# A hybrid attention and expert block on one core: low halves of the projection panels kept in DRAM, and two steps reordered

## Chip, cores and metric

The kernel runs on one core of one Trainium2 chip. The metric is the device time of one execution in microseconds; shown are single runs and their median.

## What is computed

One encoder layer on x of 1024 tokens by 1024 features, in f32, cut to what matters here:

```python
h = rms_norm(x, g_norm_mix) * (1 + sc1) + sh1
proj = h @ w_in                    # q, k, v of 8 FoX and 8 stick-breaking heads, forget logits
x = x + gt1 * (concat(norm(fox_attention), norm(sb_attention)) @ w_out)
h2 = rms_norm(x, g_norm_ffn) * (1 + sc2) + sh2
# PEER: 8 heads, per head two top-16 lists over 128 keys, then the top 16 of their sums
x = x + gt2 * sum(gelu(h2 . expert_down[e]) * gate * expert_up[e])
out = rms_norm(x, g_final)
```

## The kernel before, in words

**Two blocks and two parts.** Tokens are worked in two blocks: block A has 5 tiles of 128 tokens (in parts of 2 and 3 tiles), block B has 3. The front part (up to about 1215 us of the span) computes the adaptive weights, the projections, both attentions, the output projections and the PEER routing. The dense part (the rest) computes the experts: for block A's tokens all 128 x 128 experts as dense matmuls, for block B's tokens by gathering each token's chosen expert rows with indirect DMAs, in the background.

**Weights in two halves.** Each matmul against a weight is three matmuls (`mm3`, lines 379 to 381), of a rounded high half and the remainder. A weight panel, 128 x 1024 f32 (512 KB), is loaded as `wf` (line 329), ACT rounds it to `wh` (line 337), and DVE computes `wl = wf - wh` (line 344). Class `Panels` does this one panel ahead: `get` returns the pair that is ready, starts the next panel's rounding, puts its subtraction off by one step of the merge, and loads one more. The 24 panels of `w_in` are walked twice, by `proj(bA)` and by `proj(bB)`, so each is loaded, rounded and subtracted twice. The output and query panels (`w_out`, `w_q`) are split once, and both halves go to DRAM (line 347), from where block B reads them back (`Kept`, line 369).

**What sets the order.** In the front, Python generators yield costs, and `mrg` takes the one that is least far on, cost divided by a given total; a planner of the framework then orders each engine's instructions by the order of this code and by a timeline that it simulates. Around the change: `proj(bA)` and then `proj(bB)` (together `pp`) run as background beside the preparation of block B, attention A and the output projection of A, and after that in front, with A's routing `rA` behind. Then attention B (weight 70) and the rest of `rA` (weight 60) run beside each other. Last, output projection, routing of block B and the build of dense gates for one tile (`gbuild`).

**The attention.** `attention` (from line 580) waits until the first head pair is projected, loads its q, k and v from DRAM (lines 588 to 607), and then, turn by turn, computes scores (lines 641 to 644), softmax and stick-breaking steps on DVE and ACT, and the weighted sum (line 706).

**The dense part.** PE, DVE and ACT keep the written order there. Three expert chunks are loaded first (lines 1270 and 1272, on SP), then a chunk's down weights are split on ACT and DVE (`split_d`, lines 1289 and 1292), multiplied (`gelu_s`), weighted by the gates, and multiplied with the up weights (lines 1333 to 1335), in groups of four chunks. Between these, `sp_(n)` takes n steps of the background generator `sparse`. Its first steps are block B's candidate selection (`cands`, from line 930), three groups of 12 steps: the first seven of a group run from the copy of the indices (line 936) over eight rounds of top-16 (lines 958 to 962) to the position arithmetic (line 978); they are DVE instructions and two ACT casts (line 941). After the three groups come the gathers on POOL (lines 1221 and 1234). `PUMP_0` is 7:

```python
    for _ in range(WB):
        nextload()
    sp_(PUMP_0)
    nxt = ready.pop(0)
    split_d(nxt, True)
    split_d(nxt, False)
    gcur = loadg(0)
```

Of the kernel before, what the change touches and what calls it, by code (L numbers as in the profile page):

```python
# [11 lines left out]
F32 = mybir.dt.float32  # L12
F32R = mybir.dt.float32r
# [3 lines left out]
AF = mybir.ActivationFunctionType  # L17
# [3 lines left out]
P = 128  # L21
T = 1024
D = 1024
# [27 lines left out]
PUMP_0 = 7  # L51
# [31 lines left out]
WLP = 0  # L83
# [22 lines left out]
def tile_kernel(ctx: ExitStack, tc: tile.TileContext, x, ccol, w_ada, badac, bgt2, gcols, w_in, w_f, bf_, gout,  # L106
                w_out, w_q, keysT, edown, eup, wdense, gfin, out, dbg=None, stop=None):
    nc = tc.nc
    V, S, G, PE = nc.vector, nc.scalar, nc.gpsimd, nc.tensor
    dma = nc.sync.dma_start  # L110
# [3 lines left out]
    dram = ctx.enter_context(tc.tile_pool(name="dram", bufs=1, space=bass.MemoryType.DRAM))  # L114
# [31 lines left out]
    ksp = dram.tile([8, 2, P, T], F32R, name="ksp")  # L146
    vsp = dram.tile([8, P, T], F32, name="vsp")
    wsp = dram.tile([24, 2, P, D], F32R, name="wsp")
    gd = dram.tile([NPT * P // SB, P, NE * SB], F32, name="gd")
    gds = [dram.tile([NE * P * P, 1], F32, name="gds%d" % i) for i in range(2)]  # L150
    pidx = cst.tile([P, 1], F32, name="pidx")
# [2 lines left out]
    class Block:  # L154
        def __init__(self, t0, parts):
            self.t0, self.parts = t0, []
            i0 = 0
            for n in parts:
                self.parts.append((i0, n))
                i0 += n  # L160
            self.nt = i0
            self.ht = i0 * P
            self.nk = (t0 + i0) * P
            self.nq = 2 if t0 else 1
# [3 lines left out]
    def cols(i0, n):  # L168
        return slice(i0 * P, (i0 + n) * P)
# [70 lines left out]
    def defer(fn, n=1):  # L240
        t_ = [n, fn]
        late.append(t_)
        return t_
# [69 lines left out]
    def split(dst_h, dst_l, src):  # L313
        S.activation(dst_h, src, AF.Copy)
        V.tensor_sub(dst_l, src, dst_h.bitcast(F32))

    class Panels:
        def __init__(self, pool, srcs, bufs=3, eng=V, keep=None):
            self.eng, self.keep = eng, keep and list(keep)
            self.pool, self.src, self.bufs = pool, list(srcs), bufs  # L320
            self.ld, self.sp = [], []
            for _ in range(bufs - 1):
                self.load()
            self.split()

        def load(self):
            if self.src:
                w = self.pool.tile([P, D], F32, name="wf", tag="wf", bufs=self.bufs)
                dma(w, self.src.pop(0))
                self.ld.append(w)  # L330

        def split(self):
            if self.ld:
                w = self.ld.pop(0)
                wh = self.pool.tile([P, D], F32R, name="wh", tag="wh", bufs=2)
                wl = self.pool.tile([P, D], F32R, name="wl", tag="wl", bufs=2)
                S.activation(wh, w, AF.Copy)
                kp = self.keep.pop(0) if self.keep else None

                def low():  # L340
                    if self.eng is G:
                        G.tensor_sub(wl, w, wh.bitcast(F32))
                    else:
                        V.tensor_sub(wl, w, wh.bitcast(F32))
                    if kp is not None:
                        for n_, t_ in enumerate((wh, wl)):
                            dma(kp[n_].bitcast(F32), t_.bitcast(F32))

                self.sp.append((wh, wl, defer(low, LW)))
                self.load()  # L350
# [137 lines left out]
    def forget(b, hh, hl):  # L488
        wf = wp.tile([P, 64], F32, name="wff", tag="wff", bufs=1)
        dma(wf, w_f)  # L490
        wfh = wp.tile([P, 64], F32R, name="wfh", tag="wfh", bufs=1)
        wfl = wp.tile([P, 64], F32R, name="wfl", tag="wfl", bufs=1)
        split(wfh, wfl, wf)
        for i0, n in b.parts:
            w = n * P
            pf = pproj()
            mm3(pf[:NH, :w], wfh, wfl, hh, hl, cols(i0, n), NH)
            yield cyc(24 * w)
            fa = wp.tile([NH, HT], F32, name="fa", tag="pt", bufs=3)[:, :w]
            S.activation(fa, pf[:NH, :w], AF.Abs, bias=bft)  # L500
            S.activation(fa, fa, AF.Exp, scale=-1.0)
            S.activation(fa, fa, AF.Ln, bias=1.0)
            fm = wp.tile([NH, HT], F32, name="fm", tag="pt", bufs=3)[:, :w]
            V.tensor_scalar(fm, pf[:NH, :w], bft, 0.0, op0=OP.add, op1=OP.min)
            fc = wp.tile([NH, HT], F32, name="fc", tag="pt", bufs=3)[:, :w]
            t = b.t0 + i0
            V.tensor_tensor_scan(fc, fm, fa, 0.0 if t == 0 else fclast, op0=OP.add, op1=OP.subtract)
            if t + n < T // P:
                V.tensor_copy(fclast, fc[:, w - 1:w])
            dma(fcd[:, t * P:t * P + w], fc)  # L510
# [3 lines left out]
    done = set()  # L514

    def proj(b, hh, hl, pool):
        pan = Panels(pool, [w_in[j] for j in range(24)], bufs=2, eng=G if WLP else V)
        yield from forget(b, hh, hl)
        pend = []

# [9 lines left out]
        for pi in range(8):  # L530
            for s_ in range(3):
                wh, wl = pan.get()
                for i0, n in b.parts:
                    w, cs, gs = n * P, cols(i0, n), cols(b.t0 + i0, n)
# [45 lines left out]
    def attention(b, mixed, pool):  # L580
# [20 lines left out]
        def load_v(pi):  # L601
            vv = pool.tile([P, nk_], F32, name="vv", tag="vv")
            dma(vv, vsp[pi, :, 0:nk_])
            LV[pi] = vv
            LB[pi] = pool.tile([P, b.ht], F32R, name="qlb", tag="qlb", bufs=b.nq)
            for h_ in (la, lb):
                dma(LB[pi][h_].bitcast(F32), qsp[pi, 2, lb, qs_].bitcast(F32))
# [5 lines left out]
            yield -1  # L613
        load_kq(0)
        load_v(0)
        n = 8 * nt
        U = {}
        pair = {}
# [656 lines left out]
    def loadg(gi):  # L1275
        i1 = gi * CG
        dma = nc.sync.dma_start if gi > 1 else G.dma_start
        gg = dp.tile([P, CG, P], F32, name="gg", tag="gg", bufs=2)
        g2 = dp.tile([P, CG, P], F32, name="gg2", tag="gg2", bufs=1)
        for k in range(2):  # L1280
            dma((gg, g2)[k], gds[k].rearrange("(p c t) o -> p c (t o)", p=P, t=P)[:, i1:i1 + CG])
        g4 = dp.tile([P, NPT * P // SB, CG, SB], F32, name="g4", tag="g4", bufs=2)
        dma(g4, gd[:, :, i1 * SB:(i1 + CG) * SB].rearrange("s p (c t) -> p s c t", t=SB))
        return gg, g4, g2

    def split_d(k, act):
        if act:
            k.dh = dp3.tile([P, D], F32R, name="dh", tag="dh", bufs=2)
            S.activation(k.dh, k.wfd, AF.Copy)
        else:  # L1290
            k.dl = dp3.tile([P, D], F32R, name="dl", tag="dl", bufs=2)
            V.tensor_sub(k.dl, k.wfd, k.dh.bitcast(F32))  # L1292
# [63 lines left out]
    def sp_(n):  # L1356
        pump(n)
# [8 lines left out]

    for _ in range(WB):
        nextload()
    sp_(PUMP_0)
    nxt = ready.pop(0)  # L1370
    split_d(nxt, True)
    split_d(nxt, False)
    gcur = loadg(0)
    for gi in range(NG):
        grp = []
# [100 lines left out]
```

## Time and profile before

| | us |
|---|---|
| median of 3 runs (lowest, highest) | 3056.48 (3053.08, 3063.33) |
| the profiled execution | 3071.45 |
| its span, first to last instruction | 3069.7 |
| PE busy | 2895.8 (94%) |
| DVE busy | 2588.3 (84%) |
| ACT busy | 1189.7 (39%) |
| POOL busy | 1365.3 (44%) |

PE is the matmul engine TensorE, DVE VectorE, ACT ScalarE, POOL GpSimd, SP the queue that issues most DMAs. A time in a row is counted from the span's start. "[0.83 <-ACT qf L909]" behind an instruction says that its engine stood idle 0.83 us before it, until ACT's instruction of line 909 on tile qf let it go. L344 is line 344 of the kernel before.

### The profile page before, as it was taken

To read this page: it belongs to the slowest core of one execution; us is meant where nothing else is said; L and a number is where in the kernel's file an instruction comes from. 1 tells how busy PE (TensorE), PEld (TensorE's weight loads), DVE (VectorE), ACT (ScalarE), POOL (GpSimd) and SP (SyncE) were. 2 spreads that over 40 slices of the span, in tenths; PEclk is the share of its full clock that TensorE was granted. 3 is DMA by queue.
4 is the path that set the end of the run, shared out by engine and by line. 5 is a ranking of instruction groups with operands and counts; after the bars stand their busy time and mean duration, and the time that the engine had idled before them with its cause. 6 is when DMAs were issued, how large, how long until landed. Compare 5 with 4: busy or idle time off the path is not lost.

```text
span 3069.7 us, 48010 instructions
## 1 busy us (share of the span) xinstructions
PE 2895.8 (94%) x17472; PEld 2675.8 (87%) x17472; DVE 2588.3 (84%) x5282; ACT 1189.7 (39%) x2148; POOL 1365.3 (44%) x964
## 2 busy tenths in 40 slices
PE   5899998997989897889999999999999999999997
PEld 4899898997879897789898898998998989989986
DVE  6677554899997788889898998898989989989987
ACT  5566655445676763322132222231221222312212
POOL 0000000056756000055666665666666666666661
PEclk9999999998999998899999999999999999999998
DMA  7999454667435576379999999999999999999995
GB/s 256 285 346 280 142 198 177 211 183 197 105 82 165 217 266 241 104 277 354 350 354 339 334 355 338 344 361 347 343 344 332 346 345 342 364 332 343 340 328 196
DMA packets 368317, 856.93 MB, mean 279 GB/s; under 512 B 48952, under 2 KB 172880, under 8 KB 366032
## 3 DMA queue, kind: packets, MB, share of 16 engines
q1 hardware_dynamic: 236032, 440.08, 41.6%
q0 software_dynamic: 132048, 413.79, 38.3%
q8 instruction: 137, 2.24, 0.3%
q14 instruction: 100, 0.82, 0.1%
HBM read 742.49 MB, written 111.25 MB: 278 GB/s over the span
## 4 chain that ended last, share of the span: by engine, by line
PE 48%; DVE 22%; DMA 13%; issue 9%; ACT 4%; POOL 4%; SPq 0%; DVEq 0%; POOLq 0%; ACTq 0%
DMA ring<-in_eup,e 7%; PE sp L379 6%; PE sp L381 6%; PE sp L380 6%; DVE sacc L1239 4%; POOL ring L1234 3%; PE po L1333 3%; PE po L1335 3%; PE po L1334 3%; PE tp L1077 2%; PE av L706 2%; DMA wa<-in_w_ada 2%; PE proj L379 2%; PE pers L1333 2%; PE pers L1334 2%
## 5 line engine op out<-in xcount | busy, mean ns | idle before, releaser
L1234 POOL DMA_INDIRECT ring<-in_eup,e x384 | 557.5, 1452 | 289.7 <-DVE sacc L1239 150.3
L1221 POOL DMA_INDIRECT ring<-in_edown,e x384 | 519.2, 1352 | 373.3 <-DVE ring L1223 151.2
L379 PE MATMUL sp<-hT,dl 128*128 128x320 f32 x2048 | 636.5, 311 | 26.5 <-DVE dl L1292 16.1
L380 PE MATMUL sp<-hT,dh 128*128 128x320 f32 x2048 | 635.7, 310 | 0.0
L381 PE MATMUL sp<-hT,dh 128*128 128x320 f32 x2048 | 635.6, 310 | 0.0
L1239 DVE SCALAR_TENSOR_TENSOR sacc<-ring,sdot,sacc 128x1024 f32<-128x1024 f32 x381 | 488.2, 1281 | 66.8 <-DMA ring<-in_eup,e 62.2
L1223 DVE SCALAR_TENSOR_TENSOR ring<-ring,sx 128x1024 f32<-128x1024 f32 x384 | 460.7, 1219 | 67.2 <-DMA ring<-in_edown,e 66.1
L379 PEld LDWEIGHTS sp<-hT,dl 128*128 128x128 f32 x2048 | 387.1, 189 | 29.6 <-DVE dl L1292 15.3
L1297 ACT ACTIVATE uh<-wfu 128x1024 fp32r<-128x1024 f32 x128 | 134.8, 1053 | 680.3 <-PE po L1335 680.3
L380 PEld LDWEIGHTS sp<-hT,dh 128*128 128x128 f32 x2048 | 387.1, 189 | 1.2
L381 PEld LDWEIGHTS sp<-hT,dh 128*128 128x128 f32 x2048 | 387.0, 189 | 0.0
L1039 POOL DMA_INDIRECT gds<-g,e x128 | 238.5, 1863 | 263.0 <-DMA wf<-in_w_in 137.5
L1333 PE MATMUL po<-ul,ch 128*128 128x512 f32 x768 | 305.9, 398 | 21.1 <-DVE accB L1342 11.9
L1334 PE MATMUL po<-uh,ch 128*128 128x512 f32 x768 | 301.1, 392 | 0.0
L1335 PE MATMUL po<-uh,cl 128*128 128x512 f32 x768 | 301.1, 392 | 0.0
L1308 ACT ACTIVATE ge<-sp 128x320 f32<-128x320 f32 x256 | 110.4, 433 | 443.6 <-PE sp L381 443.5
L1333 PEld LDWEIGHTS po<-ul,ch 128*128 128x128 f32 x768 | 145.4, 189 | 66.0 <-DVE accB L1342 28.8
L1334 PE MATMUL pers<-uh,ch 128*128 128x512 f32 x512 | 199.6, 390 | 0.0
L1333 PE MATMUL pers<-ul,ch 128*128 128x512 f32 x512 | 199.5, 390 | 0.0
L1335 PE MATMUL pers<-uh,cl 128*128 128x512 f32 x512 | 199.2, 389 | 0.0
L303 POOL TENSOR_TENSOR i<-ms,mhalf 128x4 f32<-128x4 f32 (+1 forms) x16 | 22.4, 1400 | 338.7 <-DVE ms L301 338.7
L1335 PEld LDWEIGHTS po<-uh,cl 128*128 128x128 f32 x768 | 145.4, 189 | 31.2
(307 smaller groups left out, 6534.4 us busy)
## 6 DMA issues: line engine op xcount, KB each, us to landing
wfd<-in_wdense SPq DMA_DIRECT2D x128, 512.0 KB, 6.7
wfu<-in_wdense SPq DMA_DIRECT2D x128, 512.0 KB, 6.6
gd<-gt SPq DMA_DIRECT2D x16, 2048.0 KB, 8.3
g<-gd SPq DMA_DIRECT2D x30, 1024.0 KB, 14.9
wa<-in_w_ada SPq DMA_DIRECT2D x96, 256.0 KB, 5.3
wf<-in_w_in SPq DMA_DIRECT2D x48, 512.0 KB, 4.5
gds<-zt SPq DMA_DIRECT2D x32, 512.0 KB, 6.2
gg<-gds SPq DMA_DIRECT2D x60, 256.0 KB, 6.5
```

What stands on the lines that cost most here:

```text
L379: PE.matmul(pt, wl[:, c], hh[:, kd, cs], start=kd == 0, stop=False)
L380: PE.matmul(pt, wh[:, c], hl[:, kd, cs], start=False, stop=False)
L381: PE.matmul(pt, wh[:, c], hh[:, kd, cs], start=False, stop=kd == KD - 1)
L1039: G.indirect_dma_start(out=gds[nsct[0]], out_offset=off, in_=b.g[:, c_:c_ + 1], in_offset=None, compute_op=OP.add)
L1221: G.indirect_dma_start(out=r, out_offset=None, in_=edown, in_offset=bass.IndirectOffsetOnAxis(ap=bs.e[:, c_:c_ + 1], axis=0))
L1223: (V.scalar_tensor_tensor(r, r, 1.0, sx, op0=OP.mult, op1=OP.mult, accum_out=s_[:, j:j + 1]))
L1234: G.indirect_dma_start(out=r, out_offset=None, in_=eup, in_offset=bass.IndirectOffsetOnAxis(ap=bs.e[:, c_:c_ + 1], axis=0))
L1239: (V.scalar_tensor_tensor(acc, r, s_[:, j:j + 1], acc, op0=OP.mult, op1=OP.add))
L1297: S.activation(k.uh, k.wfu, AF.Copy)
L1333: PE.matmul(po, k.ch[:, tcs], k.ul[:, ds_], start=c == 0 and (gi == 0 or not per), stop=False)
L1334: PE.matmul(po, k.ch[:, tcs], k.uh[:, ds_], start=False, stop=False)
L1335: PE.matmul(po, k.cl[:, tcs], k.uh[:, ds_], start=False, stop=c == CG - 1 and (gi == NG - 1 or not per))
```

## The change

Three edits. First, a DRAM tensor `wlo` of 24 panels: in `proj(bA)` each low half is also written there after its subtraction; in `proj(bB)` the low half is loaded from there into `wl` (two buffers) beside the load of `wf`, and no subtraction is done; the rounding on ACT stays. Second, attention B yields a cost of 10 once, after its first loads and before its first scores. Third, the seven first background steps of the dense part come after the first chunk's split.

```diff
--- before.py
+++ after.py
@@ -146,6 +146,7 @@
     ksp = dram.tile([8, 2, P, T], F32R, name="ksp")
     vsp = dram.tile([8, P, T], F32, name="vsp")
     wsp = dram.tile([24, 2, P, D], F32R, name="wsp")
+    wlo = dram.tile([24, P, D], F32R, name="wlo")
     gd = dram.tile([NPT * P // SB, P, NE * SB], F32, name="gd")
     gds = [dram.tile([NE * P * P, 1], F32, name="gds%d" % i) for i in range(2)]
     pidx = cst.tile([P, 1], F32, name="pidx")
@@ -315,8 +316,9 @@
         V.tensor_sub(dst_l, src, dst_h.bitcast(F32))
 
     class Panels:
-        def __init__(self, pool, srcs, bufs=3, eng=V, keep=None):
+        def __init__(self, pool, srcs, bufs=3, eng=V, keep=None, lows=None, out=None):
             self.eng, self.keep = eng, keep and list(keep)
+            self.lows, self.out, self.wl = lows and list(lows), out and list(out), []
             self.pool, self.src, self.bufs = pool, list(srcs), bufs
             self.ld, self.sp = [], []
             for _ in range(bufs - 1):
@@ -328,13 +330,23 @@
                 w = self.pool.tile([P, D], F32, name="wf", tag="wf", bufs=self.bufs)
                 dma(w, self.src.pop(0))
                 self.ld.append(w)
+                if self.lows:
+                    wl = self.pool.tile([P, D], F32R, name="wl", tag="wl", bufs=2)
+                    dma(wl.bitcast(F32), self.lows.pop(0).bitcast(F32))
+                    self.wl.append(wl)
 
         def split(self):
             if self.ld:
                 w = self.ld.pop(0)
                 wh = self.pool.tile([P, D], F32R, name="wh", tag="wh", bufs=2)
+                if self.wl:
+                    S.activation(wh, w, AF.Copy)
+                    self.sp.append((wh, self.wl.pop(0), None))
+                    self.load()
+                    return
                 wl = self.pool.tile([P, D], F32R, name="wl", tag="wl", bufs=2)
                 S.activation(wh, w, AF.Copy)
+                lo_ = self.out.pop(0) if self.out else None
                 kp = self.keep.pop(0) if self.keep else None
 
                 def low():
@@ -342,6 +354,8 @@
                         G.tensor_sub(wl, w, wh.bitcast(F32))
                     else:
                         V.tensor_sub(wl, w, wh.bitcast(F32))
+                    if lo_ is not None:
+                        dma(lo_.bitcast(F32), wl.bitcast(F32))
                     if kp is not None:
                         for n_, t_ in enumerate((wh, wl)):
                             dma(kp[n_].bitcast(F32), t_.bitcast(F32))
@@ -514,7 +528,9 @@
     done = set()
 
     def proj(b, hh, hl, pool):
-        pan = Panels(pool, [w_in[j] for j in range(24)], bufs=2, eng=G if WLP else V)
+        low_ = [wlo[j] for j in range(24)]
+        pan = Panels(pool, [w_in[j] for j in range(24)], bufs=2, lows=low_ if b.t0 else None,
+                     out=None if b.t0 else low_)
         yield from forget(b, hh, hl)
         pend = []
 
@@ -613,6 +629,8 @@
             yield -1
         load_kq(0)
         load_v(0)
+        if b.t0:
+            yield 10.0
         n = 8 * nt
         U = {}
         pair = {}
@@ -1366,10 +1384,10 @@
 
     for _ in range(WB):
         nextload()
-    sp_(PUMP_0)
     nxt = ready.pop(0)
     split_d(nxt, True)
     split_d(nxt, False)
+    sp_(PUMP_0)
     gcur = loadg(0)
     for gi in range(NG):
         grp = []
```

## Rows read from the trace of the kernel before

**Rows 1.** The page's busy tenths in 40 equal slices, PE and DVE.

```profile
PE   5899998997989897889999999999999999999997
...
DVE  6677554899997788889898998898989989989987
```

**Rows 2.** By stretch: us, PE, PEld, DVE, ACT, POOL busy, PEclk, DMA share, GB/s.

```profile
140.00:260.00 120.00, 114.73 (x853) 112.46 (x852) 85.97 (x185) 78.17 (x185) 5.99 (x5) 1.00 1.06 338
...
580.00:690.00 110.00, 108.83 (x709) 108.25 (x707) 108.41 (x539) 49.42 (x112) 39.57 (x23) 1.00 0.62 190
...
690.00:930.00 240.00, 208.56 (x1424) 191.88 (x1424) 233.16 (x823) 159.13 (x333) 157.27 (x86) 0.90 0.50 123
...
1100.00:1200.00 100.00, 97.93 (x691) 97.08 (x689) 90.65 (x424) 53.66 (x86) 1.21 (x2) 1.00 0.68 250
...
1200.00:1320.00 120.00, 86.53 (x444) 78.85 (x444) 99.06 (x404) 36.57 (x50) 6.37 (x8) 0.84 0.37 125
```

**Rows 3.** Instructions on tile wl: the subtraction, ns min/median/max.

```profile
L344 DVE TENSOR_TENSOR wl<-wf,wh x72: 1199/1220/1230, 36.1 to 763.9; 128x1024 fp32r<-128x1024 f32 x72
```

**Rows 4.** Line 329's issues on SP, 565 to 660 us, ns; landing us.

```profile
L329 SPq DMA_DIRECT2D wf<-in_w_in x10: 328/332/333, 571.1 to 654.7; - x10
...
DMA to landing us min/median/max: 3.5/4.3/4.6
```

**Rows 5.** DMA, 140 to 260 us: packets, MB, share; count, KB, landing.

```profile
q1 hardware_dynamic: 43221, 40.37, 105.3%
...
wf<-in_w_in SPq DMA_DIRECT2D x10, 512.0 KB, 6.3
```

**Rows 6.** Waits of PE on DMA, 100 to 350 us: total us, times, longest.

```profile
PE sc L641 <- DMA qlb<-qsp: 2.5, 2, 1.4
```

**Rows 7.** ACT's timeline, last attention's start: start us, us, instruction [idle, releaser].

```profile
692.44 0.74 ACT L1016 ACTIVATE i2c<-bq 128x16 f32<-128x16 f32 x6 [3.99 <-DVE bq L999]
...
695.35 0.47 ACT L526 ACTIVATE vv<-proj 128x384 f32<-128x384 f32 x1
```

**Rows 8.** PE's timeline there; its first two rows bound one panel's 24 matmuls.

```profile
683.50 0.33 PE L379 MATMUL sc<-hT,wl 128*128 128x384 f32 x1
...
687.50 0.34 PE L381 MATMUL sc<-hT,wh 128*128 128x384 f32 x1
...
695.87 0.58 PE L379 MATMUL proj<-hT,wl 128*128 128x256 f32 x1 [6.38 <-ACT vv L526]
...
707.24 0.56 PE L641 MATMUL sc<-ka,qla 128*128 128x512 f32 x1 [2.05 <-DMA ka<-ksp]
...
712.54 0.76 PE L641 MATMUL sc<-kb,qlb 128*128 128x512 f32 x1 [3.67 <-DMA qla<-qsp]
```

**Rows 9.** DVE's timeline at the start of the dense part, same columns.

```profile
1215.79 0.27 DVE L978 SCALAR_TENSOR_TENSOR bq<-pos,bq 128x128 f32<-128x128 f32 x1
...
1217.48 0.28 DVE L890 FIND_INDEX8 i<-v,sr 128x8 uint32<-128x128 f32 x1
...
1226.15 1.23 DVE L1292 TENSOR_TENSOR dl<-wfd,dh 128x1024 fp32r<-128x1024 f32 x1 [8.39 <-ACT dh L1289]
...
1228.71 1.23 DVE L1292 TENSOR_TENSOR dl<-wfd,dh 128x1024 fp32r<-128x1024 f32 x1 [1.33 <-ACT dh L1289]
...
1255.42 0.69 DVE L1318 TENSOR_TENSOR ge<-ge,g 128x512 f32<-128x512 f32 x1 [3.23 <-ACT ge L1308]
```

**Rows 10.** SP's timeline there: the first dense load.

```profile
1217.79 0.33 SPq L1270 DMA_DIRECT2D wfd<-in_wdense  x1
```

**Rows 11.** DVE's timeline: third group's seven steps, and the split behind them.

```profile
1289.42 0.28 DVE L936 CAST ifl<-i 128x256 bf16<-128x256 uint32 x1
...
1306.34 1.22 DVE L1292 TENSOR_TENSOR dl<-wfd,dh 128x1024 fp32r<-128x1024 f32 x1
```

**Rows 12.** PE's timeline in the first dense group: its longest wait.

```profile
1288.70 0.80 PE L1333 MATMUL po<-ul,ch 128*128 128x512 f32 x1 [7.68 <-ACT accB L1340]
```

**Rows 13.** POOL's timeline: the gather from which they follow steadily.

```profile
1318.32 1.16 POOL L1221 DMA_INDIRECT ring<-in_edown,e  x1 [25.85 <-DVE g L1004]
```


## The prediction

> **What bounds the kernel now.** I read the page's busy slices first: TensorE (PE) is near full nearly everywhere and VectorE (DVE) joins it from the middle of the front part to the end [rows 1]. So the question for each stretch is which of the two has no slack, and the table of busy time by stretch answers it [rows 2]. From 140 to 260 us (projection of the first block) PE is busy 114.7 of 120 and DVE only 86.0: PE bounds, while the DMA share is 1.06, the fullest stretch outside the dense part. From 580 to 690 (projection of the second block beside routing of the first) both are full, 108.8 and 108.4 of 110. From 690 to 930 (last attention beside the rest of that routing) DVE is busy 233.2 of 240 and PE 208.6: DVE bounds. From 1100 to 1200 PE is at 97.9 of 100. At the start of the dense part, 1200 to 1320, PE falls to 86.5 of 120 and DVE does 99.1. The timelines of the two hand-overs that the change touches come next: into the last attention [rows 7, 8] and into the dense part [rows 9 to 13]. In both, PE waits for something that DVE or a queue is late with.
>
> The profiled execution took 3071.45 us (span 3069.7 and 1.75 around it), 15.0 above the median of 3056.48. The sum below is a difference, taken in that execution and added to the median. A measurement can tell about 0.3% from no change: 9 us.
>
> **Stores in the first block's projection.** Each of 24 panels now sends its low part, 512 KB, to DRAM. The subtraction stays. A store stands on SP's queue behind a new wait for that subtraction; behind it queue the next panel's load, the q, k and v spills, the adaptive weights' loads and the zero fills. Ten panel loads fall in the full stretch of 140 to 260 us, which moved 40.37 MB, 336 GB/s [rows 5]; ten stores are 5.2 MB, 15.6 us at that rate. That is the upper bound, if nothing else gives way; zero is the lower, since PE waited for DMA there only 2.5 us in 250 [rows 6]. Between them I take +4: a quarter, because PE's own waits for DMA are the nearest row, and zero fills, which nobody needs soon, share the queue and give way first. The other 14 stores meet a queue with room.
>
> Of the rate itself, the table's row shows 338 GB/s at a share above one. The Trainium skill, "DMA: Bandwidth & Descriptors", section "Bandwidth", gives 425 GB/s for a very large transfer by one core alone. By it 45.6 MB in 120 us, 380 GB/s, would still fit, the stores would cost nothing and the sum would come out 4 us lower; no stretch of this trace that I read goes that high, so the row decides.
>
> **Loads and the dropped subtraction in the second block's projection.** It removes 24 subtractions of 1.22 us each [rows 3], 1.15 from one start to the next when DVE is full, so 27.6 us of DVE work. It adds 24 loads of 512 KB on SP. The last ten panel loads of this projection go out from 571.1 to 654.7, 9.3 us apart, and land in a median of 4.3 [rows 4]. The loaded low part has two buffers, so the load for panel k+2 waits until panel k's last matmul, and has panel k+1's 9 us to land: cost nothing, covered by panel k+1; without that cover it is PE that waits.
>
> What the 27.6 us are worth depends on the place. The panels before 571 fall where DVE has room: nothing. The last ten, 11.5 us, fall where DVE is full [rows 2]. PE is full there too, so the projection can't end earlier. But at its end DVE is behind: ScalarE (ACT) waits 3.99 us for the route's indices on DVE, its copy of the last v comes at 695.35, and PE has stood 6.38 us for the buffer that this copy frees [rows 7, 8]. With 11.5 us less behind it DVE would have caught up. The last v, and with it the last attention's loads, can come 6.4 us sooner; the other 5 us come back only if DVE stays fed until 930. Bounds: 0 and -27.6. I take -10, nearest to the ten panels and a little less because the queue and ACT's order keep some.
>
> **The last attention's first turn.** Its loads are issued as before, but the merge books 10 units on it, of 70, so routing (60) gets 8.6 units first: about one panel. A panel's 24 matmuls of 384 columns run from 683.50 to 687.7, 4.2 us [rows 8], those of 256 two thirds of it: 7 us of PE put ahead of the first scores, with their DVE work behind. Nothing is added; what is moved issues no DMA but the panel's own load and spill. Today PE stands 3.67 us at the second half of the first scores for a load [rows 8]. Filling it is worth up to that; losing costs up to 7, the panel, if the attention's own chain ends the stage. I take -2, because DVE is the bound there and its order matters more than PE's.
>
> **The first dense split.** Seven steps of background work (candidate selection for one group) now come after the first split instead of before. Their DVE instructions run in written order. Before, they were mixed into the route's tail and the last ended at 1216 [rows 9], in a stretch that PE bounds [rows 2], so they cost nothing. Then DVE stood 8.39 us for the first dense weights, and the first split came at 1226.15 [rows 9]. It needs the load that goes out at 1217.79 [rows 10], just behind DVE's last route instruction [rows 9], and the change moves neither. After it, the seven steps stand bare between the first and the second split. The third group of the same work shows them alone: 1289.42 to 1306.34, 16.9 us [rows 11]. Cover: DVE's wait of 1.33 before the second split goes [rows 9]; the route's tail loses a handful of these instructions, about 1.2 us (four or five of 0.2 to 0.3 behind the last scores' arrival); and of DVE's later waits for PE, 3.23 the longest [rows 9], some 3.2 in all go. 16.9 - 1.3 - 1.2 - 3.2 = +11. PE's first chunk (48 matmuls) covers only part: it waits for the second split, and later 7.68 us on the same DVE chain as now [rows 12]. The steps' two ACT casts come behind the first split's and hold up nothing. POOL has none of it, but its steady gathers start only when DVE has done all three groups, at 1318.32 [rows 13], so they move by the same 11. Bounds: -1.2 (they still find a gap) and +16.9.
>
> Sum: +4 - 10 - 2 + 11 = +3, so 3059 us. The planner that orders the front's instructions can move each term by a few us.
>
> **Rivals.** (A) Slower: the relief doesn't reach the end. Place: the second block's projection, where PE is busy 108.8 of 110. Price: the dropped subtractions and the turn become 0, the sum is +4 + 11 = +15, 3071. It decides if the copy of the last v comes less than 3 us sooner, counted from the projection's last matmul. For it: PE shows no gap to win there. Against: the 6.38 us that PE stands right after it. (B) Faster: the stores cost nothing, all 11.5 us pass on, the attention's start gains its 6.4 on top, and the turn fills the 5.7 us that PE stands at the first scores (2.05 and 3.67 [rows 8]): 0 - 11.5 - 6.4 - 5.7 + 11 = -12.6, 3044. For it: DVE is the bound for 240 us after. Against: two of the gains may be the same time. (C) The change doesn't do what it says at the split: the steps still land in the route's tail, the sum is +4 - 10 - 2 - 1 = -9, 3047. Against it: the written order held in every case that I followed. (D) The low loads come late, 2 us for each of 24 panels: +48, 3104. Against it: 9.3 us between panels.
>
> **How the numbers follow.** Forecast 0.34, A 0.28, B 0.25, C 0.08, D 0.05. Within 0.3%: forecast and C, 0.42; faster by over 0.3%: B, 0.25; slower: A and D, 0.33. The range reaches below B and above A by some of the bounds of the stores and of the split, and leaves out D: 3038 to 3082. The likeliest case alone spans 3050 to 3066.
>
> **What would show it.** No subtraction in the second projection and DVE below 100 of 110 there; PE's stop after it shorter than 3 us; PE's DMA waits in the full stretch up by some us; the seven steps between the first and second dense split, and the first steady gather some 11 us later counted from the first split. It is wrong if the second split still follows the first within 3 us, if PE waits for low parts, or if DVE in 690 to 930 shows new idle time as large as the relief.

## The result, and the profile after

The changed kernel takes 3097.78 us (median, 3080.17 to 3099.24) against 3059.89 for the kernel before. The medians are 37.9 us apart and the means 34.0; the ratio on record for the comparison is 1.0095 (95% interval 1.0075 to 1.0116), so **slower by 29 us** (23 to 36), and all that follows goes by such ratios. 3059 was forecast, in a range that ended at 3082. The profiled execution took 3098.34 us (span 3096.5).

The table of busy time by stretch, after (us, then PE, PEld, DVE, ACT, POOL busy, granted clock, DMA share, GB/s), which answers [rows 2]:

```profile
140.00:260.00 120.00, 110.59 (x781) 105.89 (x782) 74.23 (x159) 63.50 (x151) 6.67 (x4) 1.00 1.04 342
...
580.00:690.00 110.00, 110.00 (x720) 109.83 (x720) 106.15 (x574) 52.84 (x122) 48.43 (x29) 1.00 0.78 238
...
690.00:930.00 240.00, 207.52 (x1376) 189.72 (x1376) 221.17 (x746) 153.18 (x318) 166.31 (x95) 0.89 0.51 120
...
1200.00:1320.00 120.00, 80.86 (x397) 74.08 (x398) 89.72 (x408) 34.58 (x47) 5.00 (x6) 0.79 0.34 111
```

In the second block's projection DVE fell from 108.4 to 106.2 and PE is full as before, 110.0 of 110. In the last attention and the rest of the routing, where DVE bounded with 233.2 of 240, it is now busy 221.2: 18.8 us of idle time where there were 6.8, at a granted clock of 0.89. That pair proves little, since the window is fixed and the attention's end is not. Two versions below whose code is that of the kernel before up to the tail of the route (the split's move alone, and the steps behind the second split) stood 13.1 and 16.9 us idle in it:

```profile
690.00:930.00 240.00, 213.77 (x1461) 197.19 (x1461) 226.95 (x782) 158.95 (x329) 154.84 (x85) 0.90 0.50 121
```

```profile
690.00:930.00 240.00, 215.70 (x1445) 199.79 (x1444) 223.12 (x750) 159.25 (x328) 156.55 (x87) 0.87 0.49 115
```

At the start of the dense part PE is busy 80.9 of 120 where it was 86.5, at a granted clock of 0.79.

The low parts do what they should. The instructions on tile wl, with ns least, median and most, answer [rows 3]:

```profile
L356 DVE TENSOR_TENSOR wl<-wf,wh x48: 1201/1224/1228, 36.6 to 738.3; 128x1024 fp32r<-128x1024 f32 x48
...
L358 SPq DMA_DIRECT2D wlo<-wl x24: 319/372/1130, 37.9 to 336.9; - x24
...
L335 SPq DMA_DIRECT2D wl<-wlo x24: 319/327/717, 342.9 to 659.8; - x24
```

24 of 72 subtractions are gone, 24 stores and 24 loads are there. ScalarE's timeline answers [rows 7]: the copy of the last v comes at 687.50, without a wait, 10.2 us after the projection's last matmul on a low half (677.3) where it came 14.4 after it (680.9 and 695.35). PE's stop of 6.38 us behind the projection is gone [rows 8]; its longest wait between 676 and 703 us is now 1.89.

```profile
687.50 0.47 ACT L542 ACTIVATE vv<-proj 128x384 f32<-128x384 f32 x1
```

DVE's timeline at the start of the dense part answers [rows 9]:

```profile
1212.12 0.68 DVE L904 MAX8 v<-scs 128x8 f32<-128x128 f32 x3 [11.34 <-ACT scs L897]
...
1226.64 1.23 DVE L1310 TENSOR_TENSOR dl<-wfd,dh 128x1024 fp32r<-128x1024 f32 x1 [7.41 <-ACT dh L1307]
...
1227.79 0.29 DVE L954 CAST ifl<-i 128x256 bf16<-128x256 uint32 x1
...
1244.50 0.29 DVE L996 SCALAR_TENSOR_TENSOR bq<-pos,bq 128x128 f32<-128x128 f32 x1
...
1244.78 1.23 DVE L1310 TENSOR_TENSOR dl<-wfd,dh 128x1024 fp32r<-128x1024 f32 x1
```

The route's tail has lost the seven steps and is no shorter for it: DVE stands 11.34 us for late scores, and the first split starts at 1226.64 (before: 1226.15). Then the steps stand bare from 1227.79 to 1244.78, and the second split is 16.1 us later than before. PE's timeline shows who pays, and POOL's (answering [rows 13]) that it lasts: the steady gathers start at 1334.91, 16.6 us later.

```profile
1227.92 0.63 PE L393 MATMUL sp<-hT,dl 128*128 128x320 f32 x1 [14.47 <-DVE dl L1310]
...
1246.15 0.61 PE L393 MATMUL sp<-hT,dl 128*128 128x320 f32 x1 [8.84 <-DVE dl L1310]
```

The first of the two waits was there before, the second is new:

```profile
1227.43 0.64 PE L379 MATMUL sp<-hT,dl 128*128 128x320 f32 x1 [15.16 <-DVE dl L1292]
```

POOL's row:

```profile
1334.91 1.17 POOL L1239 DMA_INDIRECT ring<-in_edown,e  x1 [25.87 <-DVE g L1022]
```

The spans differ by 26.8 us. The stretch from the first to the second split holds 15.6 of it, and 10.9 come between the ninth and the last split (1660.7 before, 1671.6 after). But that stretch is the same code in every kernel here with the old order at the split, and took 1660.7 to 1670.0 us in their profiles; in the three other versions with the steps between the splits it took 1663.5 to 1667.7. So most of the 10.9 is spread between executions, and **one pair of profiles can't say what the front did**: up to the last scores of the first attention five profiles of identical code end at 390.2 to 399.7 us, and the profile of before is the latest of them. That hides a loss in the front, which the experiments had to find by times. Below, a ratio is always to the kernel before in the same comparison, and 0.1% is 3.1 us.

### The profile page after: what moved, and what is told of

Same layout as the page of the kernel before. It is cut to its first block, busy times and chain, and to the rows that moved or that the text cites. A ratio compares the mean times of both kernels' runs of the same rounds, so it can differ in the third digit from the quotient of the medians.

```text
span 3096.5 us, 48074 instructions
## 1 busy us (share of the span) xinstructions
PE 2899.0 (94%) x17472; PEld 2671.7 (86%) x17472; DVE 2568.3 (83%) x5258; ACT 1186.3 (38%) x2148; POOL 1357.7 (44%) x964
## 3 DMA queue, kind: packets, MB, share of 16 engines
q0 software_dynamic: 132048, 413.79, 37.9%
## 4 chain that ended last, share of the span: by engine, by line
PE 44%; DVE 22%; DMA 13%; issue 11%; POOL 6%; ACT 5%; SPq 0%; DVEq 0%; POOLq 0%; ACTq 0%
DMA ring<-in_eup,e 7%; PE sp L393 4%; PE sp L394 4%; PE sp L395 4%; POOL ring L1252 4%; DVE sacc L1257 3%; PE proj L393 2%; PE proj L395 2%; PE proj L394 2%; PE tp L1095 2%; DMA ring<-in_edown,e 2%; PE av L724 2%; PE po L1351 2%; PE po L1352 2%; PE po L1353 2%
## 5 line engine op out<-in xcount | busy, mean ns | idle before, releaser
L1252 POOL DMA_INDIRECT ring<-in_eup,e x384 | 565.3, 1472 | 286.6 <-DVE sacc L1257 141.9
L1057 POOL DMA_INDIRECT gds<-g,e x128 | 223.6, 1747 | 226.5 <-DVE v L907 124.1
L1341 ACT ACTIVATE ch<-ge 128x640 fp32r<-128x640 f32 x128 | 94.5, 738 | 212.4 <-DVE ge L1336 199.6
L724 PEld LDWEIGHTS av<-vv,pt 128*128 128x128 f32 x1152 | 157.6, 205 | 17.6 <-ACT pt L738 10.3
```

Source lines behind the costliest of these rows:

```text
L724: m_ = PE.matmul(av_[:, a, i, :], pt[:, q * P:(q + 1) * P], vv[:, kb_ * P + a * 64:kb_ * P + a * 64 + 64], start=kb_ == 0, stop=kb_ == qt)
L1057: G.indirect_dma_start(out=gds[nsct[0]], out_offset=off, in_=b.g[:, c_:c_ + 1], in_offset=None, compute_op=OP.add)
L1252: G.indirect_dma_start(out=r, out_offset=None, in_=eup, in_offset=bass.IndirectOffsetOnAxis(ap=bs.e[:, c_:c_ + 1], axis=0))
```

## The experiments

**The parts of the change, each undone or alone.** Theory at this point: the moved steps are the whole loss. Rivals: the stores lose part of it in the front; the turn eats the relief. The steps put back ahead of the split:

```diff
         nextload()
+    sp_(PUMP_0)
     nxt = ready.pop(0)
     split_d(nxt, True)
     split_d(nxt, False)
-    sp_(PUMP_0)
```

> The changed kernel with the seven steps of background work put back ahead of the first dense split; stores, loads of low parts and the turn stay. Theory (the moved steps are the whole loss, 16.6 us bare between the first and second split, and the rest nets to nothing): second split again within 3 us of the first, first split within 4 us of 1226 us, time 16 to 28 us below the changed kernel, so within 9 us of the kernel before. Rival 1 (part of the loss is made in the front, by the stores): still 10 us or more above the kernel before, first split later than 1232. Rival 2 (the longer dense part, 1813 us from first to last split against 1786, is not the steps' doing): the dense part stays 10 us longer than before even with the second split within 3 us of the first.

Ratio 1.0038 (1.0022 to 1.0053), 11.6 us above the kernel before. The second split follows the first by 2.6 us. The split's part is 1.0095 - 1.0038, 17 us, and **the rest is not zero**: the theory falls. The first rival's time came, its sign did not: the first split is at 1221.0, not behind 1232. The second falls, as the way from the first split to the last is 6 us longer than in the profile before, not 10.

```diff
-        if b.t0:
-            yield 10.0
```

> The changed kernel without the turn booked on the last attention; stores, loads and the moved split stay. Theory (the last attention is bound by its own chain, the relief of VectorE becomes idle time there with or without the turn): first split within 4 us of 1226, time within 6 us of the changed kernel. Rival (the turn eats the relief, since it puts routing ahead of the attention that sets the end): first split 8 to 20 us sooner, before 1219, and the time lower by the same.

Ratio 1.0062 (1.0043 to 1.0080): 10 us below the changed kernel. The theory named 6, the rival a first split before 1219; it came at 1221.0. The turn costs. With both edits undone, only the stored low parts are left:

> Only the stored low parts: no turn, and the seven steps ahead of the first split as before. Theory (relief becomes idle time, the stores hide): within 6 us of the kernel before, the scores of the first attention some 9 us later as in the changed kernel and the first split within 4 us of 1226. Rival 1 (the relief is real and the turn ate it): 8 to 20 us below the kernel before. Rival 2 (the stores cost more than the loads give back): 5 to 15 us above it, with the first split later by that.

Ratio 1.0002 (0.9987 to 1.0017): stores and loads together are worth between 4 us less and 5 us more, as the theory had it by time. Its first split did not come within 4 us of 1226 but at 1215.9; the version above, whose code is the same up to there but for the tail, had it at 1221.0, so one profile says little here too. And the split's move alone, on the kernel before:

> The kernel before with the moved split alone, which is the seven steps behind the first dense split. Theory (the steps stand bare): second split 16 to 17 us later than the first's usual place, time 16 to 18 us above the kernel before; 25 to 28 above it if the later drift in the dense part is the steps' doing too. Rival (the move is hidden, the loss is made by the stores): within 5 us of the kernel before.

Ratio 1.0065 (1.0045 to 1.0085), 20 us (14 to 26): the theory's 16 to 18 lie in the interval, and the rival falls. Its DVE timeline, first and second split:

```profile
1219.99 1.23 DVE L1292 TENSOR_TENSOR dl<-wfd,dh 128x1024 fp32r<-128x1024 f32 x1 [7.11 <-ACT dh L1289]
...
1238.12 1.23 DVE L1292 TENSOR_TENSOR dl<-wfd,dh 128x1024 fp32r<-128x1024 f32 x1
```

18.1 us apart where 2.6 were: 15.5 of the 20 us are in sight there. From low parts alone to low parts and turn to the changed kernel the steps are +0.6, +11.0 and +17.4 us. These add up by construction; but in the other order the split costs 18.4 (the second of these runs less the third) and the turn 10.1.

**What the stores cost and the loads bring.**

```diff
-        low_ = [wlo[j] for j in range(24)]
+        low_ = [wlo[0]] + [None] * 23
...
-                     lows=low_ if b.t0 else None,
+                     lows=[wlo[0]] * 24 if b.t0 else None,
```

> No turn, the seven steps ahead of the first split as before. The first block's projection stores one panel's low part instead of 24, and the second block's projection loads that one for every panel, so its subtractions are gone and its loads are all there (which leaves the low parts of 23 panels out of the computation). Theory (the stores cost what the relief gives back): the first scores of the first attention come at 94 to 97 us as in the kernel before, and the time is 6 to 14 us below the kernel before. Rival (the relief is worth nothing, it turns into idle time of VectorE in the last attention): within 4 us of the kernel before.

Ratio 1.0003 (0.9986 to 1.0020), as the rival had it: what the loads free is, at best, a few us by the end.

```diff
-        pan = Panels(pool, [w_in[j] for j in range(24)], bufs=2, lows=low_ if b.t0 else None,
-                     out=None if b.t0 else low_)
+        pan = Panels(pool, [w_in[j] for j in range(24)], bufs=2, out=None if b.t0 else low_)
```

> No turn, steps as before; the first block's projection stores all 24 low parts and nobody reads them, the second block's subtracts as before. Theory (the stores delay the first block's first panels): first scores at 103 to 106 us, time 6 to 12 us above the kernel before. Rival (the stores are free by the end, the 9 us at the first scores are made up in the rest of the projection): within 4 us of the kernel before.

Ratio 1.0034 (1.0020 to 1.0049), 10 us, as the theory had it. The first scores come at 102.0 us (in the kernels without all stores 91.7 to 96.2, in those with them 102.0 to 105.7). But that is not a wait for the stores. The written order is another one: PE has 381 matmuls ahead of the first scores in every version with all the stores, and 325 in every version without. From the start to the first scores, stores alone and the kernel before (the last of its 326 is the first score):

```profile
0.00:102.00 102.00, 66.01 (x381) 55.27 (x382) 67.11 (x129) 53.80 (x105) 5.99 (x18) 0.97 0.83 288
```

```profile
0.00:94.90 94.90, 60.17 (x326) 50.16 (x327) 62.58 (x120) 48.02 (x94) 5.99 (x18) 0.93 0.77 263
```

In the stretch of 200 to 250 us, where the queue was full before, PE does 44.68 instead of 48.32 us while the rate is no higher (first the stores alone, then the kernel before); none of PE's waits there ends on a DMA.

```profile
200.00:250.00 50.00, 44.68 (x314) 42.32 (x314) 30.52 (x65) 26.28 (x62) 3.17 (x2) 1.00 1.03 335
```

```profile
200.00:250.00 50.00, 48.32 (x361) 47.50 (x360) 35.41 (x77) 32.23 (x80) 2.33 (x2) 1.00 1.06 348
```

```diff
-        low_ = [wlo[j] for j in range(24)]
+        low_ = [wlo[j] if j >= 12 else None for j in range(24)]
```

(and a panel without one is not loaded)

> Stored low parts for the last 12 of the 24 panels alone, where VectorE is full in the second block's projection; the first 12 are subtracted in both. No turn, steps as before. Theory (the stores' cost is made at the first panels, the relief at the last ten): first scores at 94 to 97 us, time 5 to 12 us below the kernel before. Rival (relief and cost are both spread evenly over the panels): half of each, within 4 us of the kernel before and of the version with all 24.

Ratio 0.9985 (0.9968 to 1.0002). The order ahead of the first scores is that of the kernel before again, they are back at 95.4, and the same stretch, in which this version's stores have begun, is at

```profile
200.00:250.00 50.00, 48.51 (x361) 47.52 (x360) 35.05 (x79) 32.11 (x80) 3.24 (x2) 1.00 1.05 353
```

so the cost goes with the stores of the first twelve panels. Whether these cost by the queue or by the order that the planner writes with them, no run here separates. Measured once more beside the next group:

> The version with the last 12 low parts stored, no turn, steps as before, once more, as the partner of the two versions above that are built on it. Theory (half the stores keep the relief and lose the cost): 2 to 10 us below the kernel before, again. Rival (it is the kernel before within the measurement): within 2 us of it.

Ratio 0.9973 (0.9954 to 0.9993). Over both, 5 to 8 us below the kernel before, at the theory's lower end, as if the relief were kept and the stores' cost lost. Against so plain a sum speaks that the loads alone gained nothing. The three full versions (1.0003, 1.0034, 1.0002) don't add up, by 10 us where their intervals allow some 8; the written order differs in each, and the next group shows what that alone is worth.

**The turn.** On the kernel before, alone:

> The kernel before with the turn alone. Theory (the turn puts some 8 us of routing ahead of the attention, which ends the stage, whether or not VectorE was relieved): 5 to 12 us above the kernel before, the scores of the last attention ending 4 to 9 us later counted from its first. Rival (the turn costs only with the relief, because then the routing runs out of work sooner): within 4 us of the kernel before.

Ratio 1.0022 (1.0007 to 1.0038), 7 us; from the last attention's first scores to its last 221.3 us where the kernel before had 208.0, more than the 4 to 9 us that were expected. The theory: it puts some 8 us of routing ahead of an attention that ends the stage. Two versions test that on the one with twelve low parts, where it takes 205.8 and 211.1 us:

```diff
-TOT_B = 70.0
+TOT_B = 80.0
```

> The version with the last 12 low parts stored, no turn, and the opposite of the turn: the last attention's total in the merge is 80 units instead of 70, so that it is put ahead of the routing by an eighth all along. Theory (the attention's own chain of turns ends the stage, what is put ahead of it costs and what is put behind it gains): the last scores 4 to 10 us sooner counted from the first ones, time 3 to 10 us below the version with 70. Rival (VectorE's sum of work is the bound, order costs only when the routing runs out too soon): the attention ends sooner and the routing's rest stands bare behind it, time within 4 us of the version with 70, or above.

```diff
+        if b.t0:
+            yield 20.0
```

> The version with the last 12 low parts stored, and a turn of 20 units instead of none (10 in the change). Theory (each 10 units put some 8 us of routing ahead of an attention that ends the stage): 14 to 22 us above the version without a turn, the last scores 15 to 25 us later counted from the first. Rival (a turn costs a fixed sum, by the panel put ahead of the first scores): 7 to 12 us above it, as with 10 units.

Ratios 0.9960 (0.9939 to 0.9980) and 0.9964 (0.9946 to 0.9983), beside 0.9973 for their partner. The first agrees with the theory, 4 us below its partner with the stage at 200.4 us, though intervals of 6 us can't tell it from its rival. The second was to lose 14 to 22 us, or 7 to 12 by its rival. **A turn of 20 units costs nothing, and the theory falls**, with that rival. What the stage shows instead is in its busy time. These are the windows from first to last scores: low parts alone, the same with the turn of 10, the kernel before with the turn of 10, and (a run below) the kernel before with 20:

```profile
701.80:912.60 210.80, 192.16 (x1296) 175.52 (x1296) 203.00 (x693) 144.64 (x291) 130.53 (x72) 0.90 0.50 123
```

```profile
699.60:915.90 216.30, 189.56 (x1253) 172.74 (x1254) 204.89 (x684) 142.84 (x292) 150.39 (x84) 0.88 0.51 120
```

```profile
701.00:922.30 221.30, 199.02 (x1265) 183.21 (x1266) 204.85 (x700) 144.68 (x296) 136.34 (x74) 0.85 0.48 118
```

```profile
706.50:901.50 195.00, 173.65 (x1237) 157.95 (x1235) 193.21 (x662) 142.94 (x284) 120.10 (x61) 0.96 0.51 128
```

DVE has 193 to 205 us of work in the stage; what it stands idle is 7.8, 11.4, 16.5 and 1.8 us, and the granted clock is 0.90, 0.88, 0.85 and 0.96. Differences of a few us are spread: the version with twelve low parts stood 5.2 and 10.0 us idle in two profiles of one code. The same order of the stage in other versions gives 10.4 beside the 7.8, 15.4 beside the 11.4, and 5.8 to 7.6 in three profiles of the kernel before's. From the longest of the four, windows around a fall of the clock:

```profile
830.00:840.00 10.00, 9.12 (x72) 8.02 (x70) 10.00 (x35) 7.13 (x12) 6.26 (x5) 1.00 0.86 208
...
840.00:844.50 4.50, 1.50 (x9) 1.02 (x9) 4.50 (x12) 2.61 (x5) 3.96 (x2) 1.00 0.61 180
...
844.50:865.00 20.50, 20.43 (x90) 19.85 (x91) 15.00 (x47) 11.54 (x27) 1.00 (x1) 0.50 0.02 1
```

PE was busy 9.12 of 10 us and then 1.50 of 4.5, with waits of 1.56 us at most; then the clock fell to 0.50, the lower of its two levels (1.2 GHz). For 20.5 us PE was busy nearly all the time at that speed, and DVE, the engine that bounds the stage, waited for it, as its timeline says:

```profile
860.77 0.56 DVE L674 TENSOR_SCALAR t<-sc 128x384 f32<-128x384 f32 x1 [3.27 <-PE sc L646]
```

The Trainium skill, "TensorE: Matmul & The Clock Gate", section "A second HAM failure mode: psum-queue depth-cycling", tells of a kernel whose TensorE stood often and briefly between groups of matmuls and swung between its two levels; the rows agree in that much. How much of the idle time the clock explains differs by version. On the kernel before with the turn of 10, 13.1 of DVE's 16.5 us fall while the clock is at the lower level; in the changed kernel only 4.7 of 15.4. So there the order makes DVE wait at the full clock too, and by what is not shown. Four more versions asked whether 10 units are dear by themselves.

```diff
+        if b.t0:
+            yield 10.0
```

> The version with the last 12 low parts stored and the turn of 10 units. Theory (the turn of 10 writes an order in which TensorE is underfed and its granted clock falls, VectorE then stands): 6 to 12 us above the version without a turn, VectorE idle for over 11 us between the first and the last scores of the last attention (10.0 without a turn, 3.3 with 20). Rival (the turn costs only with all 24 or none of the low parts stored, by chance of the order): within 4 us of the version without a turn.

Ratio 0.9984 (0.9968 to 1.0000), DVE idle 6.5 us although the granted clock is 0.89: 10 units are not dear here, the rival holds, and a low clock alone is not the price.

> The version with the last 12 low parts stored and a turn of 5 units. Theory (the order decides, not the size; what it costs is read from VectorE's idle time in the last attention): anything from 10 us below to 10 above the version without a turn, but in step with that idle time, some 1 us for each us. Rival (a price by size): half of what 10 units cost, 3 to 6 us above.

Ratio 0.9962 (0.9947 to 0.9977), idle 8.3 us: no price by size. Whether it goes in step with the idle time, as the theory had it, can't be told beside the 5.2 and 10.0 of its partner.

> The kernel before with a turn of 20 units. Theory (20 units write a better order whatever is stored): 0 to 8 us below the kernel before, granted clock in the last attention 0.92 or more. Rival (each version draws its own order): anything, 5 us or more above the kernel before would show it.

Ratio 0.9972 (0.9957 to 0.9988), 9 us below the kernel before, with the clock at 0.96, about as the theory had it.

```diff
         if b.t0:
-            yield 10.0
+            yield 20.0
```

> The changed kernel with 20 units in place of 10, nothing else. Theory (the loss of the turn goes with the order that 10 units write): 10 to 18 us below the changed kernel, so 12 to 20 above the kernel before, which is the moved split's price. Rival (the turn's loss stays or doubles): as the changed kernel, 27 or more above the kernel before.

Ratio 0.9992 (0.9980 to 1.0003). One number changed, **the changed kernel is 31 us faster and level with the kernel before**, more than the theory's 10 to 18. Is the split's price gone too? The steps put back:

> The changed kernel with a turn of 20 units and the seven steps ahead of the first split: all low parts stored, only the order at the split as in the kernel before. Theory (the moved steps stand bare whatever goes before): second split within 3 us of the first, 14 to 22 us below the same version with the steps moved, so 16 to 26 below the kernel before. Rival (with the earlier front the steps have room): within 5 us of the same version with the steps moved.

Ratio 0.9978 (0.9960 to 0.9995): the split costs only 4 us here, give or take 7, at the rival's end, although with the steps moved the second split still comes 18.1 us after the first. PE's timelines tell why: the last scores of the route, and the first dense matmul, with the steps in the tail and then without:

```profile
1190.50 0.94 PE L895 MATMUL proj<-kt,qf 128*128 128x128 f32 x6 [0.58 <-ACT qf L927]
...
1213.41 0.64 PE L393 MATMUL sp<-hT,dl 128*128 128x320 f32 x1 [21.98 <-DVE dl L1310]
```

```profile
1183.43 0.94 PE L895 MATMUL proj<-kt,qf 128*128 128x128 f32 x6 [0.58 <-ACT qf L927]
...
1195.55 0.64 PE L393 MATMUL sp<-hT,dl 128*128 128x320 f32 x1 [11.19 <-DVE dl L1310]
```

With them PE waits 21.98 us, because DVE, which has the steps to do, ends the tail 12 us behind the last scores (at 1202.8, the last of the steps at 1201.04); without them 6 behind (1189.2), and PE waits 11.19. The first dense matmuls are 17.9 us apart; 6.8 of that is spread, since the two profiles are as far apart at the last instruction of DVE before their code first differs (1132.4 and 1125.6). The other 11 us come from the tail. So here the tail does give most of the steps' time back. In the kernel before it did not: there DVE ended the tail 6 us behind the last scores with the steps in it (1211.34 and 1217.8).

**The steps behind the second split**, on the kernel before:

```diff
-    sp_(PUMP_0)
...
                 split_d(nxt, False)
+            if gi == 0 and c == 0:
+                sp_(PUMP_0)
```

> The kernel before with the seven steps put behind the second dense split instead of ahead of the first. Theory (VectorE has no room anywhere in the first dense group, so the steps cost their own time wherever they stand): second split within 3 us of the first, third or fifth split 12 to 17 us later than in the kernel before counted from the first, time 12 to 18 us above it. Rival (the cost came from TensorE's wait for the second split; once it has two chunks in hand, they cover the steps): fifth split no more than 6 us later, time within 7 us of the kernel before.

Ratio 1.0065 (1.0044 to 1.0086), 20 us again, as the theory had it within the interval. DVE's timeline, the first two splits, the first step and the third split:

```profile
1219.85 1.23 DVE L1292 TENSOR_TENSOR dl<-wfd,dh 128x1024 fp32r<-128x1024 f32 x1 [7.49 <-ACT dh L1289]
...
1222.40 1.23 DVE L1292 TENSOR_TENSOR dl<-wfd,dh 128x1024 fp32r<-128x1024 f32 x1 [1.33 <-ACT dh L1289]
...
1223.55 0.29 DVE L936 CAST ifl<-i 128x256 bf16<-128x256 uint32 x1
...
1252.42 1.22 DVE L1292 TENSOR_TENSOR dl<-wfd,dh 128x1024 fp32r<-128x1024 f32 x1
```

The third split stands 32.6 us behind the first where it stood 15.7: 16.9 us, the whole of the steps. DVE has no room in the first dense group, with one chunk in PE's hand or two.

## Why the prediction was wrong

**The first dense split: the right mechanism, mis-sized.** The text had the steps bare between the splits, [rows 11] gave their 16.9 us, and they took 17.0. The failing step is the cover, "16.9 - 1.3 - 1.2 - 3.2 = +11". Only the first, 1.33 before the second split, was there. The 3.2 of later waits did not go (the third split is 16.0 us later, the ninth 16.8), since those waits belong to a chain that moved along as a whole: the longest is there again, 16.5 us later than in [rows 9].

```profile
1271.96 0.69 DVE L1336 TENSOR_TENSOR ge<-ge,g 128x512 f32<-128x512 f32 x1 [3.23 <-ACT ge L1326]
```

The 1.2 of the tail did not come either, as DVE stood waiting for scores there. The price is 15.6 us in the traces; by times 17 to 20. What the times have above 15.6 is within their intervals, with the tail: from the last attention's last scores to the first split it was 1.7 to 4.1 us longer without the steps in three pairs of profiles. That a tail bound by DVE would have given more of it back is shown by the versions with a turn of 20.

**The turn: -2 was forecast, +7 to +11 came**, and the working was wrong too: "7 us of PE put ahead of the first scores". The first scores were not late: with the low parts 21.8 us after the projection's last matmul with the turn, 21.9 without. The loss is inside the attention, where the new order made DVE wait: on the kernel before mostly for a PE at the lower clock, in the changed kernel mostly at the full clock, for a reason that stays open. The bounds (3.67 us to be won, 5.7 in rival B, and 7 to be lost) priced a shift of work and not an order: by the runs 10 units cost between about nothing and 11 us, and 20 units gain 9 on the kernel before.

**Stores and relief: -6 forecast, +0.6 measured.** The sum failed; how it falls on its two terms is not settled. In the version with the stores alone they cost 10 us, not 4, and the loads beside them give back 9.8, as forecast; in the version with the loads alone the relief is worth nothing.

What the traces say of the stores: identical code ends the first attention at 390.2 to 399.7 (mean 395.2), the seven versions with all the stores at 399.8 to 403.0 (mean 401.2), so +6 there. The +4 was sized by waits for the queue in the full stretch, and the sign that was named for it did not come: PE's waits for DMA from 100 to 350 us went from 2.5 us to none. The zero fills gave way, as assumed (24 in the full stretch where there were 27), and with nine stores in it the stretch moved 40.95 MB for 40.37 [rows 5]:

```profile
q1 hardware_dynamic: 39755, 40.95, 103.9%
...
gds<-zt SPq DMA_DIRECT2D x24, 512.0 KB
...
wlo<-wl SPq DMA_DIRECT2D x9, 512.0 KB
```

Yet PE did 4.1 us less in it, and all of its waits there end on ACT and DVE. What the working left out is that stores change the order that the planner writes; the 9 us at the first scores go with 56 more matmuls put ahead of them. The Trainium skill, "DMA: Bandwidth & Descriptors", section "Where 436 GB/s comes from", says that in transfers between HBM and SBUF the HBM side binds, at some 358 GB/s per core. The full stretch, which holds stores too, agrees, at 342; the fullest 50 us of these traces, in the dense part of the version with stores alone, moved 371, a little above. The 425 GB/s of that page's table, on which the prediction weighed a zero, showed nowhere.

What they say of the relief: the last v came 4.2 us sooner and PE's 6.38 us were gone, so the rival's condition "less than 3 us sooner" was not met. DVE in the projection's last stretch fell to 106.2 of 110 and not below 100, since routing filled most of the time. In the last attention DVE stood idle 7.8 and 10.4 us with the low parts alone, beside 5.8 to 7.6 before; so of the case that the prediction named as proof against itself ("new idle time as large as the relief") a few us at most are seen.

**The rivals.** A, with relief lost, had 3071: its +15 was right in kind, though its condition was not met. C fell (18.1 us between the splits), and D too: no wait of PE ends on a stored low part. None had the turn on the dear side beyond its 7 us. The range added the bounds of the stores and of the split by "some of"; with the split at its own upper bound (+16.9), the turn at its (+7) and the relief at 0 with +4 for the stores it would have been +28, about what came.

**What stays open:** why 10 units write an order that makes DVE wait with 24 low parts or none and not with twelve, and 20 units don't. Every version with a turn of 10 has its routing ahead (DVE reads the first block's last route scores at 783 to 787 us, without a turn at 792 to 813, with 20 at 754 to 772), the cheap ones too, so that alone is not the cause. Open, too, are how the first twelve stores cost, and how stores and relief share their sum.

## What to carry to other kernels

Put background work on the bounding engine only where a trace shows it idle, and take as its price its own time: idle time that ends on a chain of which the moved work becomes a link is no cover. Where a planner writes the order of a stage, an edit of a priority is a draw of a new order, worth 10 us either way here; try several values before any is judged, and read the result from times first: the bounding engine's idle time in that stage says where to look, but differed by 5 us between two profiles of one code. Store what is read back only for the items that the relief needs: with the last twelve panels the kernel was 5 to 8 us faster than before, with all of them level.

Versions faster than both kernels came out of it: twelve low parts with the attention at 80 units (0.9960), with a turn of 5 (0.9962) or of 20 (0.9964), the old order at the split in all.

## What the runs showed of the hardware that was not expected

A fall of TensorE's clock without any long wait before it (1.50 of 4.5 us busy, no wait over 1.56), with 20.5 us at the lower level behind it, in a stage whose bound was another engine; and that two written orders of such a stage differ by 26 us (221.3 and 195.0 from first to last scores), 15 of them in that engine's idle time and the rest in the work that falls into the stage.
